# A 1 KB store of expert 0's first values, issued on GpSimd's DMA ring ahead of the full store

## The chip, the cores and the metric

One Trainium2 chip, one of its cores. The metric is the device time of one execution in microseconds (us). The kernel before takes 183.33 us (median of 5 runs, 183.1 to 183.47). A change of the median under about 0.2% (0.37 us) can't be told from no change here.

## What is computed

Eight experts, each a two-layer network with a ReLU between, for 256 rows each:

```python
n_experts, capacity, hidden, expert_hidden = 8, 256, 512, 2048
h = np.matmul(x, w1)      # (8, 256, 512) x (8, 512, 2048)
h = np.maximum(h, 0)
return np.matmul(h, w2)   # (8, 256, 2048) x (8, 2048, 512), float32
```

All inputs and the output are float32 in HBM. w1 and w2 are 4 MB each for every expert, 64 MB in all; the output is 4 MB.

## The kernel before

**Loads.** Each expert's w1 and w2 goes from HBM to SBUF in one DMA (`load_w1`, line 70; `load_w2`, line 76), which turns float32 into bf16 on the way, so 4 MB are read and 2 MB written (2048 KB in the profile). The last two experts' w2 come in pieces: w2(6) in two halves, w2(7) in six pieces of 5, 4, 3, 2, 1 and 1 sixteenths. w1 and w2 have three buffers each, so w1(3) may be loaded only when the first layer of expert 0 has used w1(0), and so on. Nearly all of these, the x of the last four experts and all stores but the last expert's, are issued by GpSimd (POOL in the profile) and share one ring, q0 in the profile. The x of the first four experts goes through SP's queue at the start, and the last expert's result through SP's and ACT's queues at the end (lines 194 and 195).

**Work.** For each expert TensorE transposes x (line 86; the copies of the result are lines 93 and 95), does the first layer (line 105, 64 matmuls, whose results ACT and DVE bring through the ReLU into SBUF in turns, lines 115 and 113), then the second layer (line 125, 32 matmuls into two PSUM tiles). DVE copies the first of the two to the output tile (line 136), ACT the second (line 137). An output tile holds two experts, 1 MB; there are three such buffers. `store` (line 140) writes one from SBUF to HBM.

**Order.** The order on every engine is the order of the calls, written out by hand (lines 143 to 195). GpSimd's instructions run in that order, and a DMA that must wait holds up every one behind it. The scheduler puts in the waits; DMAs from GpSimd take eight completion semaphores in turn, so a DMA also waits until the one eight before it has landed. The calls around the change are these, with their issue in the order of the ring:

```python
    first_layer(0)
    load_w1(3)
    transpose_x(1)
    second_layer(0)
    load_w2(3)        # line 163
    first_layer(1)
    load_w1(4)
    transpose_x(2)
    second_layer(1)
    load_w2(4)
    store(0, 1)       # line 169
    first_layer(2, ...)
    load_w1(5)        # line 171
```

So the ring holds, in order: w1(0), w2(0), w1(1), w2(1), x of experts 4 to 7, w1(2), w2(2), w1(3), w2(3), w1(4), w2(4), store(0, 1), w1(5), w1(6), w1(7), w2(5), store(2, 3), the two halves of w2(6), the six pieces of w2(7), store(4, 5), store(6).

Of the kernel before, what the change touches and what calls it, by code (L numbers as in the profile page):

```python
# [10 lines left out]
def kernel(  # L11
# [7 lines left out]
    nc = tc.nc  # L19
# [20 lines left out]
    out_r = out.rearrange("e (p mt) n -> p e mt n", p=P)  # L40
# [11 lines left out]
    w1_sb, w2_sb, ht, o_sb = {}, {}, {}, {}  # L52
# [19 lines left out]
    def load_w2(e):  # L72
        w2_sb[e] = wpool.tile([P, KT2, H], bf, tag="w2", name="w2_sb")
        cuts = {E - 2: (0, 8, 16), E - 1: (0, 5, 9, 12, 14, 15, 16)}.get(e, (0, KT2))
        for lo, hi in zip(cuts, cuts[1:]):
            nc.gpsimd.dma_start(w2_sb[e][:, lo:hi, :], w2_r[e, :, lo:hi, :])  # L76

    def transpose_x(g, kts=range(KT1)):


        n = GROUPS[g][1]
        J = n * MT
        for kt in kts:
            pt = ps_o.tile([P, J, P], bf, tag="ps_o", name="pt_tr")
            for j in range(J):
                nc.tensor.transpose(pt[:, j, :], x_b[g][:, j, kt::KT1], identity[:])  # L86
            src = pt[:].rearrange("p (j m) (e l) -> p m e l j", m=MT, e=n)
            for mt in range(MT):
                dst = xt[g][:, kt, :, mt * P:(mt + 1) * P].rearrange(
                    "p e (l j) -> p e l j", j=J // MT  # L90
                )
                if mt % 2:
                    nc.scalar.copy(dst, src[:, mt])  # L93
                else:
                    nc.vector.tensor_copy(dst, src[:, mt])  # L95

    def first_layer(e, between=()):
        g = group_of[e]
        xe = xt[g][:, :, e - GROUPS[g][0], :]
        ht[e] = hpool.tile([P, KT2, C], bf, tag="ht", name="ht_sb")  # L100
        for q in range(KT2 // 2):
            ph = ps_h.tile([P, 2, C], f32, tag="ps_h", name="pt_h")
            for i in range(2):
                for kt in range(KT1):
                    nc.tensor.matmul(  # L105
                        ph[:, i, :],
                        w1_sb[e][:, kt, 2 * q + i::KT2],
                        xe[:, kt, :],
                        start=(kt == 0),
                        stop=(kt == KT1 - 1),  # L110
                    )
            if q % 2:
                nc.vector.tensor_relu(ht[e][:, 2 * q:2 * q + 2, :], ph[:])  # L113
            else:
                nc.scalar.activation(ht[e][:, 2 * q:2 * q + 2, :], ph[:], relu)  # L115
            if q % 2 and between:
                between.pop(0)()

    def second_layer(e):
        po = [  # L120
            ps_o.tile([P, H], f32, tag="ps_o", name=f"pt_o{mt}") for mt in range(MT)
        ]
        for kt in range(KT2):
            for mt in range(MT):
                nc.tensor.matmul(  # L125
                    po[mt][:],
                    ht[e][:, kt, mt * P:(mt + 1) * P],
                    w2_sb[e][:, kt, :],
                    start=(kt == 0),
                    stop=(kt == KT2 - 1),  # L130
                )
        es = next(es for es in STORES if e in es)
        if e == es[0]:
            o_sb[es] = opool.tile([P, 2, MT, H], f32, tag="o", name="out_sb")
        o = o_sb[es][:, e - es[0]]
        nc.vector.tensor_copy(o[:, 0, :], po[0][:])  # L136
        nc.scalar.copy(o[:, 1, :], po[1][:])  # L137

    def store(*es):
        nc.gpsimd.dma_start(out_r[:, es[0]:es[-1] + 1], o_sb[es][:, :len(es)])  # L140


    nc.sync.dma_start(x_f[:, :2], x[0:2].rearrange("e (p mt) k -> p e mt k", p=P))
# [16 lines left out]
    load_w1(3)  # L160
    transpose_x(1)
    second_layer(0)
    load_w2(3)
    first_layer(1)
    load_w1(4)
# [3 lines that stand above are left out]
    store(0, 1)  # L169
    first_layer(2, [lambda kt=kt: transpose_x(3, [kt]) for kt in range(KT1)])  # L170
    load_w1(5)
# [5 lines left out]
    load_w1(7)  # L177
    load_w2(5)
    store(2, 3)
    load_w2(6)  # L180
    second_layer(4)
# [5 lines left out]

    second_layer(5)
    store(4, 5)
    second_layer(6)  # L190
    store(6)
# [34 lines left out]
```

## Time and profile before

| | before |
|---|---|
| median of 5 runs | 183.33 us (183.1 to 183.47) |
| the profiled execution: its time | 183.47 us |
| its span, first to last instruction | 181.3 us |
| PE busy | 127.4 us (70%) |
| DVE, ACT, POOL busy | 32.8, 33.9, 15.8 us |
| moved by DMA | 41.01 MB, mean 226 GB/s |
| mean granted TensorE clock | 0.945 |

The profile is of one execution on the chip; times in it count from the start of its span. Busy time of an engine leaves out waits. A DMA has an issue (the instruction on POOL, SP or ACT) and a landing (its completion); "DMA to landing" is the time between the start of the one and the other, so a landing's time is the issue's start plus that. Where DMAs stand in one ring, the distance from one landing to the next is the time that the later one took of the ring. The chain of work that ended last follows what released each step, back from the end.

### The profile page before, as it was taken

Reading aid. Unit: us, or ns where it says so; the run is one execution under the profiler, and the core shown is the slowest. Engines: PE = TensorE matmul, PEld = TensorE weight load, DVE = VectorE, ACT = ScalarE, POOL = GpSimd, SP = SyncE. Lnnn points to the kernel's source line nnn. Section 1 sums busy time; section 2 is a strip of 40 time slices with the busy share of each in tenths; the row PEclk is TensorE's granted clock in tenths of the full one; section 3 lists DMA queues with packets and bytes.
Section 4 is the critical chain, followed back from the end, with each engine's and each line's share of the span. In section 5 each row is a group of like instructions: output and inputs, shape, how many; then the busy total and the mean of one; then the engine's idle time right before and its main releaser. Section 6 shows DMA issues by size and latency. Waiting matters only on the chain.

```text
span 181.3 us, 1891 instructions
## 1 busy us (share of the span) xinstructions
PE 127.4 (70%) x832; PEld 89.8 (50%) x832; DVE 32.8 (18%) x56; ACT 33.9 (19%) x61; POOL 15.8 (9%) x33
## 2 busy tenths in 40 slices
PE   0200898979690299969987692925979498997980
PEld 0100685469340189427933681404969386443430
DVE  0100023033401025211311130010324123010110
ACT  2403323023301025111301130011223022010110
POOL 7200001010102000100010006011010101110100
PEclk9999999999999579996999999996999979999996
DMA  6998998999899989998999899999999999999994
GB/s 187 333 260 202 231 231 174 231 231 231 175 230 231 231 174 231 231 231 174 231 231 228 177 231 296 229 213 228 202 224 213 228 199 310 229 212 213 206 350 176
DMA packets 4984, 41.01 MB, mean 226 GB/s; under 512 B 496, under 2 KB 752, under 8 KB 2672
## 3 DMA queue, kind: packets, MB, share of 16 engines
q0 software_dynamic: 4272, 38.27, 95.6%
q1 hardware_dynamic: 560, 2.36, 3.6%
q10 hardware_dynamic: 144, 0.26, 0.4%
q8 instruction: 6, 0.10, 0.2%
q14 instruction: 2, 0.02, 0.0%
HBM read 71.30 MB, written 4.19 MB: 416 GB/s over the span
## 4 chain that ended last, share of the span: by engine, by line
DMA 44%; PE 42%; another core or an unknown queue 8%; issue 1%; ACT 1%; POOL 1%; DVE 1%; POOLq 0%
DMA w_sb<-in_w_dram 44%; PE pt_o L125 23%; PE pt_h L105 18%; PE pt_tr L86 1%; ACT xt L93 1%; DVE ht_sb L113 0%; ACT out_sb L137 0%; POOL w_sb L76 0%; POOL w_sb L70 0%; DVE xt L95 0%; POOL identity masks.py:199 0%; POOL identity masks.py:197 0%; POOLq L210 0%
## 5 line engine op out<-in xcount | busy, mean ns | idle before, releaser
L105 PE MATMUL pt_h<-xt,w_sb 128*128 128x256 bf16 x512 | 67.2, 299 | 32.9 <-DMA w_sb<-in_w_dram 21.9
L105 PEld LDWEIGHTS <-w_sb 128*128 128x128 bf16 x512 | 60.9, 148 | 39.9 <-DMA w_sb<-in_w_dram 35.1
L125 PE MATMUL pt_o<-w_sb,ht_sb 128*128 128x512 bf16 x256 | 56.6, 379 | 9.1 <-DMA w_sb<-in_w_dram 6.8
L125 PEld LDWEIGHTS <-ht_sb 128*128 128x128 bf16 x256 | 24.9, 98 | 39.1 <-issue 8.9
L113 DVE TENSOR_SCALAR ht_sb<-pt_h 128x512 bf16<-128x512 f32 x32 | 22.1, 692 | 78.6 <-PE pt_h L105 78.6
L115 ACT ACTIVATE ht_sb<-pt_h 128x512 bf16<-128x512 f32 x32 | 19.1, 598 | 60.3 <-PE pt_h L105 60.3
L137 ACT COPY out_sb<-pt_o 128x512 f32<-128x512 f32 x8 | 4.7, 586 | 61.0 <-PE pt_o L125 61.0
L136 DVE COPY out_sb<-pt_o 128x512 f32<-128x512 f32 x8 | 5.5, 692 | 58.1 <-PE pt_o L125 58.1
L76 POOL DMA_DIRECT2D w_sb<-in_w_dram x14 | 7.6, 541 | 58.6 <-DMA w_sb<-in_w_dram 33.2
L70 POOL DMA_DIRECT2D w_sb<-in_w_dram x8 | 4.5, 558 | 82.8 <-PE pt_h L105 51.0
L86 PE MATMUL pt_tr<-identity,x_b 128*128 128x128 bf16 x64 | 5.1, 231 | 6.7 <-ACT x_b L153 6.7
L86 PEld LDWEIGHTS <-x_b 128*128 128x128 bf16 x64 | 4.6, 117 | 6.8 <-ACT x_b L153 6.7
L95 DVE COPY xt<-pt_tr 128x128 bf16<-128x128 bf16 (+2 forms) x16 | 5.6, 382 | 7.1 <-PE pt_tr L86 7.1
L93 ACT COPY xt<-pt_tr 128x128 bf16<-128x128 bf16 (+2 forms) x16 | 5.2, 378 | 8.1 <-DVE xt L95 8.1
L140 POOL DMA_DIRECT2D out_dram<-out_sb x4 | 2.7, 678 | 13.2 <-ACT out_sb L137 12.9
L156 ACT CAST x_b<-x_f 128x1024 bf16<-128x1024 f32 x2 | 2.0, 1042 | 8.9 <-DMA x_f<-in_x_dram 8.9
L153 ACT CAST x_b<-x_f 128x1024 bf16<-128x1024 f32 x1 | 1.0, 1044 | 3.6 <-DMA x_f<-in_x_dram 3.6
L153 ACT ACT_TABLE_LOAD x1 | 1.3, 1283 | 0.7 <-PEq L210 0.7
L154 ACT CAST x_b<-x_f 128x1024 bf16<-128x1024 f32 x1 | 1.0, 1042 | 0.0
L66 POOL DMA_DIRECT2D x_b<-in_x_dram x1 | 0.6, 558 | 0.0
masks.py:199 POOL TENSOR_SCALAR_AFFINE_SELECT identity<-identity 128x128 bf16<-128x128 bf16 x1 | 0.3, 290 | 0.1
masks.py:197 POOL MEMSET identity<- 128x128 bf16 x1 | 0.2, 224 | 0.0
(4 smaller groups left out, 0.4 us busy)
## 6 DMA issues: line engine op xcount, KB each, us to landing
w_sb<-in_w_dram POOLq DMA_DIRECT2D x14, 2048.0 KB, 47.8
out_dram<-out_sb POOLq DMA_DIRECT2D x3, 1024.0 KB, 46.0
x_f<-in_x_dram SPq DMA_DIRECT2D x2, 1024.0 KB, 10.1
w_sb<-in_w_dram POOLq DMA_DIRECT2D x2, 1024.0 KB, 51.6
x_b<-in_x_dram POOLq DMA_DIRECT2D x1, 1024.0 KB, 48.5
w_sb<-in_w_dram POOLq DMA_DIRECT2D x1, 640.0 KB, 49.1
w_sb<-in_w_dram POOLq DMA_DIRECT2D x1, 512.0 KB, 46.5
out_dram<-out_sb POOLq DMA_DIRECT2D x1, 512.0 KB, 9.0
```

Of the source, the lines that this page charges most:

```text
L70: nc.gpsimd.dma_start(w1_sb[e][:], w1_r[e])
L76: nc.gpsimd.dma_start(w2_sb[e][:, lo:hi, :], w2_r[e, :, lo:hi, :])
L86: nc.tensor.transpose(pt[:, j, :], x_b[g][:, j, kt::KT1], identity[:])
L93: nc.scalar.copy(dst, src[:, mt])
L95: nc.vector.tensor_copy(dst, src[:, mt])
L105: nc.tensor.matmul(ph[:, i, :], w1_sb[e][:, kt, 2 * q + i::KT2], xe[:, kt, :], start=(kt == 0), stop=(kt == KT1 - 1),)
L113: nc.vector.tensor_relu(ht[e][:, 2 * q:2 * q + 2, :], ph[:])
L115: nc.scalar.activation(ht[e][:, 2 * q:2 * q + 2, :], ph[:], relu)
L125: nc.tensor.matmul(po[mt][:], ht[e][:, kt, mt * P:(mt + 1) * P], w2_sb[e][:, kt, :], start=(kt == 0), stop=(kt == KT2 - 1),)
L136: nc.vector.tensor_copy(o[:, 0, :], po[0][:])
L137: nc.scalar.copy(o[:, 1, :], po[1][:])
L140: nc.gpsimd.dma_start(out_r[:, es[0]:es[-1] + 1], o_sb[es][:, :len(es)])
```

## The change

One more DMA is issued on GpSimd, between second_layer(0) and load_w2(3): 16 partitions by 16 float32 values (64 bytes of each partition) of expert 0's first output half go from the output tile to the same place in HBM where store(0, 1) writes them again later. So that the two writes can't cross, store(0, 1) is made to wait until the small one has landed.

```diff
     def store(*es):
-        nc.gpsimd.dma_start(out_r[:, es[0]:es[-1] + 1], o_sb[es][:, :len(es)])
+        d = nc.gpsimd.dma_start(out_r[:, es[0]:es[-1] + 1], o_sb[es][:, :len(es)])
+        if 0 in es:
+            tc.add_manual_dep(
+                d.ins,
+                early.ins.name,
+                mybir.DependencyInfo(
+                    mybir.DependencyClass.Sync, mybir.DependencyReason.SCHED_ONLY
+                ),
+                reason="overwrites it",
+            )
...
     second_layer(0)
+    early = nc.gpsimd.dma_start(out_r[0:16, 0, 0, 0:16], o_sb[(0, 1)][0:16, 0, 0, 0:16])
     load_w2(3)
```

In the built program, PE, DVE, ACT and SP have the same instructions in the same order as before. POOL has one more. Its waits are: the small store waits for DVE's copy (line 136 for expert 0); store(0, 1) now also waits for the small store's landing and, because the turn of the semaphores has moved by one, for the landing of x of experts 4 to 7; the second-layer copies of expert 6 on DVE and ACT, which take over store(0, 1)'s buffer, wait for the small store too. The DMAs behind store(0, 1) keep their own waits or move to one that an earlier DMA of the same ring had already met.

## The prediction, made before the changed kernel was run

> **What bounds the kernel.** I read the page's DMA part first: is the ring ever short of work?
>
> ```profile
> DMA  6998998999899989998999899999999999999994
> q0 software_dynamic: 4272, 38.27, 95.6%
> ```
>
> The 16 DMA engines are busy in every slice, and GpSimd's ring (q0) alone fills 95.6% of their span. PE is busy for 70%. So the ring is the limit; what counts for the end is how much time a DMA takes of the ring, not when it was issued, as long as it is issued before the ring comes to it. Next, POOL's part of the timeline gives the issues around the change (columns: start, duration, engine, line, and in brackets the idle time before with its releaser).
>
> ```profile
> 29.06 0.54 POOL L70 DMA_DIRECT2D w_sb<-in_w_dram  x1 [23.38 <-PE pt_tr L86]
> 37.34 0.53 POOL L76 DMA_DIRECT2D w_sb<-in_w_dram  x1 [7.74 <-PE pt_o L125]
> 45.55 0.53 POOL L70 DMA_DIRECT2D w_sb<-in_w_dram  x1 [7.68 <-PE pt_tr L86]
> 55.10 0.53 POOL L76 DMA_DIRECT2D w_sb<-in_w_dram  x1 [9.03 <-PE pt_o L125]
> 55.94 0.71 POOL L140 DMA_DIRECT2D out_dram<-out_sb  x1 [0.30 <-issue]
> 72.79 0.56 POOL L70 DMA_DIRECT2D w_sb<-in_w_dram  x1 [16.14 <-PE pt_h L105]
> 91.01 0.53 POOL L70 DMA_DIRECT2D w_sb<-in_w_dram  x1 [17.66 <-PE pt_h L105]
> ```
>
> In order these are w1(3), w2(3), w1(4), w2(4), store(0, 1), w1(5), w1(6). The view of one line in a window around one issue gives its time to landing; here w1(3) and then store(0, 1):
>
> ```profile
> L70 POOL DMA_DIRECT2D w_sb<-in_w_dram x1: 536/536/536, 29.1 to 29.1; - x1
> DMA to landing us min/median/max: 52.7/52.7/52.7
> ```
>
> ```profile
> L140 POOL DMA_DIRECT2D out_dram<-out_sb x1: 714/714/714, 55.9 to 55.9; - x1
> DMA to landing us min/median/max: 58.6/58.6/58.6
> ```
>
> Every DMA waits some 50 us in the ring behind others. From the same view for each: w2(2) lands at 5.11 + 66.9 = 72.0, w1(3) at 29.06 + 52.7 = 81.8, w2(3) at 37.34 + 54.1 = 91.4, w1(4) at 45.55 + 55.6 = 101.15, w2(4) at 55.10 + 56.9 = 112.0, store(0, 1) at 55.94 + 58.6 = 114.5, w1(5) at 72.79 + 51.4 = 124.2. One 2048 KB load takes 9.7 us of the ring, the store 2.5. Last, the end of the chain that ended last:
>
> ```profile
> 109.24 44.00 DMA w_sb<-in_w_dram
> 153.24 0.04 issue
> 153.28 7.07 PE pt_o L125 x32
> 160.34 0.25 another core or an unknown queue
> 160.60 0.04 issue
> 160.64 3.61 PE pt_o L125 x16
> 164.25 1.20 another core or an unknown queue
> 165.45 0.04 issue
> 165.50 10.58 PE pt_o L125 x48
> 176.08 0.02 issue
> 176.10 0.59 ACT out_sb L137
> ```
>
> The 44 us are w2(5)'s way through the ring. PE then stops for 0.25 and 1.20 us, and starts at once when each half of w2(6) has landed: the second half was issued at 112.30 and took 53.2, so 165.5. After that PE runs 10.58 us without a stop. So **the end is the landing of w2(6)'s second half plus 10.58 us of PE and the last copy and store**. Whatever the ring loses before 165.5 is added to the end one for one; a ring that gained more than 1.20 + 0.25 us would find PE in the way.
>
> **The change, part by part.**
>
> *The small store's issue on POOL.* It waits for DVE's copy of expert 0, which the timeline has at 36.86 for 0.69, so until 37.55; load_w2(3) went at 37.34 before. The other issues take 0.53 to 0.71 us, so w2(3) is issued at about 37.55 + 0.25 of release + 0.6 = 38.4, some 1.1 us later. The ring comes to it when w1(3) is done, at 81.8: 43 us of cover. The next issue, w1(4), waits for PE until 45.55 and isn't touched. Cost 0; without the cover it would be 1.1 us.
>
> *The small store in the ring.* It stands between w1(3) and w2(3) and takes ring time of every DMA engine it uses. No row has a 1 KB DMA. The nearest: the last two 128 KB pieces of w2(7) land at 153.52 + 21.2 = 174.7 and 156.03 + 19.4 = 175.4, the piece before them at 143.83 + 30.2 = 174.0, so each takes 0.70 us; by bytes it should be 9.7 x 128/2048 = 0.61. So 0.1 us goes with being a DMA at all. x of experts 4 to 7 (1024 KB) says the same: it lands 4.9 us after w2(1), and half of 9.7 is 4.85. Bounds: from 0 (what two landings can hide in their rounding) to 0.7, if the smallest DMA seen is a floor. I take **0.1**, since both rows have it, and nothing but the bytes differs.
>
> A rule that speaks against the change stands in the Trainium skill, page "DMA: Bandwidth & Descriptors", section Specifications: pieces under 512 bytes are not moved at line rate but by a read-modify-write. The same page (section "Anatomy of one DMA") puts a fixed 2.0 us on a DMA, most of it the receipt of the write. If that fixed part held the ring, the sum would be +2.0 us; the landings above, 0.1 over the bytes, say that it overlaps with what follows for large pieces, and no row here shows pieces of 64 bytes to HBM.
>
> *The wait of store(0, 1).* It now waits for the small store's landing, just behind w1(3)'s: 81.8 + 0.1 = 81.9 instead of 55.94. Behind it on POOL stands w1(5), then issued at about 82.6 instead of 72.79; w1(6) waits for PE until 91.01 as before. The ring reaches the store at 112.0, when w2(4) is done: 30 us of cover; w1(5) needs the ring at 114.5: 32 us. Cost 0; uncovered, it would be the 26 us of delay. Its other new wait, x of experts 4 to 7, is met at 4.06 + 48.5 = 52.6. The copies of expert 6 on DVE and ACT come after 168 us, when the small store has long landed: 0. All that comes later keeps its waits in substance: 0.
>
> *Sum.* 181.3 + 0.1 = 181.4 of span; with the 183.47 - 181.3 = 2.2 us around it 183.57 for the profiled execution, which lay 0.14 above the median. So the median goes from 183.33 to **183.4**.
>
> **The rivals.**
>
> *The first write to the output costs something, and the small store takes it over more cheaply.* The ring has two odd intervals. w2(4), the load right before the first store, took 112.0 - 101.15 = 10.85 us, 1.15 over the rest; a window set on each shows it:
>
> ```profile
> 91.10:100.80 9.70, 7.07 (x32) 3.03 (x31) 1.03 (x2) 0.59 (x1) 0.44 (x1) 1.00 1.01 216
> 100.80:111.70 10.90, 7.21 (x64) 7.04 (x65) 2.77 (x4) 2.39 (x4) 2.32 (x4) 1.00 1.01 235
> ```
>
> Nothing of the kind stands before store(2, 3): w2(5) landed 9.7 after w1(7). If the surplus belongs to a first write, 1 KB may pay less of it than 1 MB. At most the whole 1.15 is saved: 183.33 + 0.1 - 1.15 = 182.3; half of it: 182.9. Against it: w1(1) lands at 38.0, 10.65 after w2(0) (2.47 + 24.9 = 27.4), with no store in sight, so a surplus of 1 us has other causes too; and POOL issues four DMAs in a row from 108.72 in just that stretch, which the change leaves alone.
>
> *The small store stalls the ring itself (slower).* One mechanism: on each DMA engine a 64-byte write to HBM holds the ring until it is through, between w1(3) and w2(3), at 81.8. Its price from the rows: the 0.7 of the smallest DMA, or the 1.15 of the ring's surplus beside the first store, if that is what a first write costs and it comes twice. 183.33 + 0.7 = 184.0, with both the 0.1 and 1.15, 184.6. It decides from 0.37 us on, as no cover stands between the ring and the end. For it: pieces of 64 bytes are not in the profile at all. Against: store(0, 1) itself has no stall behind it, as w1(5) lands 9.7 after it.
>
> *The wait of store(0, 1) drains the ring (slower).* This needs the small store to land after 112, 30 us later than its place in the ring. Price then: all of what it is late. I see nothing for it.
>
> *Nothing comes of it,* as the small store is too small to see: that is the forecast with 0 for 0.1, and the same case.
>
> **How the numbers follow.** Forecast (0 to 0.3 us more, 183.2 to 183.7 with the spread of medians): 0.42. The first write's cost moved and reduced: 0.25, faster by over 0.2%. The small store's stall: 0.31, and the drained ring 0.02: slower. So faster 0.25, same 0.42, slower 0.33, and 183.4 as the likeliest. Range: to 184.6, the slow rival's upper price; below to 182.5, which takes in three quarters of the saving. What it leaves out is the rest of the saving and of the drained ring, about 0.15. The forecast's own range is 183.2 to 183.7.
>
> **What would show it.** Right: w1(3) lands at 81.8 and w2(3) 9.7 to 9.9 us later; POOL issues store(0, 1) at about 82 and w1(5) right behind; w2(4) keeps its 10.85; w2(6)'s second half lands at 165.5 to 165.7. The faster rival: w2(4)'s interval falls to about 9.7, w2(3)'s grows by less. The slower: w2(3) takes 10.4 us or more and nothing is given back. The forecast is wrong from the start if w2(3)'s or w2(4)'s interval moves by more than 0.4 us.

## The result, and the profile after

The changed kernel takes 182.90 us (median of 32 runs, 182.62 to 183.61), the kernel before 183.33 us (median of 55). The ratio is 0.998, 95% interval [0.9975, 0.9986]: faster by about 0.2% (0.43 us), where 0.1 us more was forecast.

The first surprise is in two numbers. The profiled execution of the changed kernel took 183.20 us, with this first line of its page:

```profile
span 181.4 us, 1893 instructions
```

The span is 0.1 us longer than before (181.3), and so the execution should be 0.1 us slower; yet it is 0.27 faster. 183.20 - 181.41 leaves 1.79 us around the span, where before 183.47 - 181.30 left 2.17. Within the span everything went as forecast. The DMA rows of the page, first:

```profile
DMA  5998998999899989998999898999999999999994
q0 software_dynamic: 4304, 38.28, 95.5%
```

The ring is as full as before; it has 32 packets more (4304 against 4272), one of 64 bytes and one of 4 bytes on each of 16 DMA engines; the trace has such a 4-byte packet on every engine for each of the ring's DMAs (432 for 27 before), and the sixteen of 64 bytes took 24 ns each. POOL's timeline around the change (start, duration, engine, line, idle time before with its releaser):

```profile
27.79 0.54 POOL L70 DMA_DIRECT2D w_sb<-in_w_dram  x1 [22.11 <-PE pt_tr L86]
36.57 0.51 POOL L172 DMA_DIRECT2D out_dram<-out_sb  x1 [8.24 <-DVE out_sb L136]
37.07 0.55 POOL L76 DMA_DIRECT2D w_sb<-in_w_dram  x1
47.33 0.53 POOL L70 DMA_DIRECT2D w_sb<-in_w_dram  x1 [9.71 <-PE pt_tr L86]
56.03 0.53 POOL L76 DMA_DIRECT2D w_sb<-in_w_dram  x1 [8.16 <-PE pt_o L125]
82.70 0.72 POOL L140 DMA_DIRECT2D out_dram<-out_sb  x1 [26.14 <-DMA out_dram<-out_sb]
83.41 0.56 POOL L70 DMA_DIRECT2D w_sb<-in_w_dram  x1
```

The small store is the second row. store(0, 1) now stands idle for 26.14 us, released by the small store's landing, and w1(5) goes right behind it, both some 10 to 27 us later than before. w1(5) lands at 83.41 + 40.9 = 124.31 (before 124.19), so this costs nothing beyond the 0.1 us by which the whole chain lies later. The view of the small store's line in the changed kernel:

```profile
L172 POOL DMA_DIRECT2D out_dram<-out_sb x1: 512/512/512, 36.6 to 36.6; - x1
DMA to landing us min/median/max: 45.4/45.4/45.4
```

It lands at 36.57 + 45.4 = 81.97. By the same view w1(3) lands at 27.79 + 54.0 = 81.79, w2(3) at 37.07 + 54.4 = 91.47, w1(4) at 47.33 + 53.9 = 101.23, w2(4) at 56.03 + 56.1 = 112.13, store(0, 1) at 82.70 + 31.9 = 114.60. The views of w1(3) and of w2(3) in the changed kernel, and of w2(3) before:

```profile
L70 POOL DMA_DIRECT2D w_sb<-in_w_dram x1: 536/536/536, 27.8 to 27.8; - x1
DMA to landing us min/median/max: 54.0/54.0/54.0
```

```profile
L76 POOL DMA_DIRECT2D w_sb<-in_w_dram x1: 554/554/554, 37.1 to 37.1; - x1
DMA to landing us min/median/max: 54.4/54.4/54.4
```

```profile
L76 POOL DMA_DIRECT2D w_sb<-in_w_dram x1: 528/528/528, 37.3 to 37.3; - x1
DMA to landing us min/median/max: 54.1/54.1/54.1
```

w2(3) stands 9.68 us behind w1(3), exactly as before (91.44 - 81.76). Over the profiled executions of all the kernels of this document but the one with many pieces, the distance is 9.67 to 9.78 in the nine without a store there and 9.68 to 9.79 in the four with the 1 KB store. So the small store takes none of the ring's time that landings can show. The long interval of w2(4) is still there as well, 10.90 us; the windows of the changed kernel over w1(4) and w2(4) (columns as before: the stretch, its length, each engine's busy time, clock, DMA share, GB/s):

```profile
91.10:100.80 9.70, 7.07 (x32) 3.03 (x31) 0.69 (x1) 0.59 (x1) 0.00 (x0) 1.00 1.01 216
100.80:111.70 10.90, 7.21 (x64) 7.04 (x65) 2.77 (x4) 2.39 (x4) 2.32 (x4) 0.96 0.99 230
```

And the last rows of the chain that ended last:

```profile
165.56 0.04 issue
165.60 10.56 PE pt_o L125 x48
176.16 0.02 issue
176.18 0.59 ACT out_sb L137
```

From w2(5)'s issue on (109.26, before 109.24) it is row by row the chain of before, up to 0.1 us later. Nothing in it could make the kernel faster. What is left is the time around the span.

### The profile page after: what moved, and what is told of

It reads as the page before. It is cut to its first block, busy times and chain, and to the rows that moved or that the text cites. A ratio compares the mean times of both kernels' runs of the same rounds, so it can differ in the third digit from the quotient of the medians.

```text
span 181.4 us, 1893 instructions
## 1 busy us (share of the span) xinstructions
PE 129.4 (71%) x832; PEld 90.0 (50%) x832; DVE 32.8 (18%) x56; ACT 33.9 (19%) x61; POOL 16.3 (9%) x34
## 3 DMA queue, kind: packets, MB, share of 16 engines
q0 software_dynamic: 4304, 38.28, 95.5%
## 4 chain that ended last, share of the span: by engine, by line
DMA 44%; PE 42%; another core or an unknown queue 8%; issue 1%; POOL 1%; DVE 1%; ACT 1%; POOLq 0%
DMA w_sb<-in_w_dram 44%; PE pt_o L125 23%; PE pt_h L105 18%; PE pt_tr L86 1%; DVE ht_sb L113 0%; ACT out_sb L137 0%; POOL w_sb L76 0%; POOL w_sb L70 0%; ACT xt L93 0%; DVE xt L95 0%; POOL identity masks.py:199 0%; POOL identity masks.py:197 0%; POOLq L220 0%
## 5 line engine op out<-in xcount | busy, mean ns | idle before, releaser
L105 PE MATMUL pt_h<-xt,w_sb 128*128 128x256 bf16 x512 | 66.3, 296 | 30.1 <-DMA w_sb<-in_w_dram 19.1
L105 PEld LDWEIGHTS <-w_sb 128*128 128x128 bf16 x512 | 60.2, 148 | 36.8 <-DMA w_sb<-in_w_dram 32.3
L125 PE MATMUL pt_o<-w_sb,ht_sb 128*128 128x512 bf16 x256 | 59.3, 391 | 9.9 <-DMA w_sb<-in_w_dram 8.6
L125 PEld LDWEIGHTS <-ht_sb 128*128 128x128 bf16 x256 | 25.6, 100 | 42.0 <-issue 15.1
L140 POOL DMA_DIRECT2D out_dram<-out_sb x4 | 2.7, 681 | 39.1 <-DMA out_dram<-out_sb 26.1
L172 POOL DMA_DIRECT2D out_dram<-out_sb x1 | 0.5, 512 | 8.2 <-DVE out_sb L136 8.2
## 6 DMA issues: line engine op xcount, KB each, us to landing
out_dram<-out_sb POOLq DMA_DIRECT2D x3, 1024.0 KB, 31.9
```

The lines of the kernel that those rows point to most:

```text
L105: nc.tensor.matmul(ph[:, i, :], w1_sb[e][:, kt, 2 * q + i::KT2], xe[:, kt, :], start=(kt == 0), stop=(kt == KT1 - 1),)
L125: nc.tensor.matmul(po[mt][:], ht[e][:, kt, mt * P:(mt + 1) * P], w2_sb[e][:, kt, :], start=(kt == 0), stop=(kt == KT2 - 1),)
L140: d = nc.gpsimd.dma_start(out_r[:, es[0]:es[-1] + 1], o_sb[es][:, :len(es)])
```

## The experiments

### Is the gain outside the span, and which part of the change brings it?

**Theory A:** the span is unchanged, and the time around it has fallen. **Theory B:** the one pair of numbers from before is a stray, and the gain lies in the span. Every run has a time and a span, so the two can be told apart by repeating both kernels and by taking the change apart.

The kernel before, unchanged:

> The kernel before, unchanged, to have several of its executions with their spans. Ratio 1.000 to itself within 0.1%. Theory A (the 0.43 us of the changed kernel lie outside the span, since its profiled pair 183.20 / 181.41 leaves 1.79 us around the span where the one pair of before, 183.47 / 181.30, leaves 2.17): the executions here have 2.15 us or so around a span of 181.1 to 181.2. Theory B (the gain lies in the span, and the one pair of before is a stray): 1.8 us around a span of about 181.5.

Measured: 183.41 us, ratio to the other runs of itself 1.0007 [0.9994, 1.0019]; median span 181.2, and in its 12 runs 2.12 to 2.22 us around it, median 2.17. Over the 89 runs of the kernel before that stood beside the experiments: median span 181.1, around it 2.11 to 2.24, median 2.17; the experiments ran on three chips, and on each of them the kernel before has 2.17 or 2.18. Spans are given to 0.1 us, which is most of that width.

The changed kernel, unchanged:

> The changed kernel, unchanged, on the same chip as the two that take it apart. Both theories: 0.998 (0.997 to 0.999), span about 181.1, 1.8 us around it.

Measured: 182.87 us, ratio 0.9984 [0.997, 0.9998]; median span 181.1, around it 1.74 to 1.83, median 1.78. In the 33 runs of the changed kernel's own result it is 1.74 to 1.84, median 1.79, with the same span of 181.1. **Theory A holds**: the spans agree, and the 0.38 us between 2.17 and 1.79 accounts for the gain, which is 0.35 to 0.43 us by the medians of the times. The two ranges don't touch.

The small store without the wait of store(0, 1):

```diff
     second_layer(0)
+    early = nc.gpsimd.dma_start(out_r[0:16, 7, 0, 0:16], o_sb[(0, 1)][0:16, 0, 0, 0:16])
     load_w2(3)
...
-    nc.sync.dma_start(out_r[:, 7, 0, :], o[:, 0, 0, :])
+    d = nc.sync.dma_start(out_r[:, 7, 0, :], o[:, 0, 0, :])
+    tc.add_manual_dep(d.ins, early.ins.name, ..., reason="waits for it")
```

> The small store alone: the same 16 by 64 bytes at the same place in the ring, but to expert 7's rows in HBM, which the last store on SP overwrites some 90 us later (that one waits for it, at no cost). store(0, 1) and w1(5) are issued early again. If the store itself or its place in the ring brings the gain: 0.998. If the later issue of store(0, 1) and w1(5) brings it: 1.000 or 1.001 (the ring's 0.1 us).

Measured: 183.21 us, ratio 1.0002 [0.999, 1.0013]; span 181.2, around it 2.01 to 2.07, median 2.04.

The wait without the small store:

```diff
-    load_w1(3)
+    early = load_w1(3)       # load_w1 returns its DMA
...
     def store(*es):
+        if 0 in es: add_manual_dep(d.ins, early.ins.name, ..., reason="waits for it")
```

> The wait alone: no small store; store(0, 1) waits until w1(3) has landed (81.8), so that it and w1(5) are issued at about 82 and 83 as in the changed kernel. If the later issue brings the gain: 0.997 to 0.998, since the ring's 0.1 us is not paid either. If the small store brings it: 1.000.

Measured: 183.20 us, ratio 0.9997 [0.9986, 1.0008]; span 181.2, around it 1.99 to 2.10, median 2.02.

Neither part gives the gain: each run came out as if the other part brought it, so both accounts missed. But both moved the time around the span, to values of their own, 2.04 and 2.02. So in these kernels it is a property of the program, steady from run to run, and it moves while the spans agree. What these programs differ in, apart from the ring, is the number of instructions, waits counted, in POOL's stream. The page's instruction counts and the trace's records of each engine show it: 1891 before, 60 of them on POOL; 1893 in the changed kernel, 62 on POOL (the store and one more wait, where the part on the change counts the store alone); 1893 with the store alone (61 on POOL, and one more wait on SP); 1890 with the wait alone (59 on POOL, one wait fewer).

### Is it the length of POOL's stream?

**Theory L:** the time around the span goes with the length of POOL's stream, whatever the instructions are. **Theory S:** it goes with the small store, its DMA, its turn of semaphores or its wait. The test adds memsets, instructions that fill a tile with a value; here the tile is one value that nothing reads, so they do nothing for the result and touch no DMA:

```diff
     identity = const.tile([P, P], bf, name="identity")
+    spare = [const.tile([1, 1], f32, name=f"spare{i}") for i in range(2)]
...
     make_identity(nc, identity)
+    for t in spare:
+        nc.gpsimd.memset(t[:], 0.0)
```

> The kernel before with two memsets of one value each on POOL, beside the identity at the start: no DMA, no wait, no store; POOL's stream is as long as in the changed kernel, two instructions more than before. Theory L (what changed is the time outside the span, and it goes with the length of POOL's stream of instructions): time 182.9, 1.8 us around a span of 181.1. Theory S (it goes with the small store, its DMA or its wait): 183.2 to 183.4, 2.17 us around.

Measured: 183.01 us, ratio 0.9987 [0.9975, 0.9999]; median span 181.2, around it 1.76 to 1.84, median 1.80. **Two empty memsets bring what the small store brought.** The first line of its page has the same count as the changed kernel, with no small store in it; the profiled execution was one with a long span, 0.8 us over the median of before:

```profile
span 181.9 us, 1893 instructions
```

Its time was 183.66, so again 1.78 around: what happens in the span comes and goes by some tenths from run to run, and the time around it doesn't follow.

One memset, `range(1)`:

> The same with one memset: POOL's stream has one instruction more than before, as in the kernel with the small store but without store(0, 1)'s wait. Theory L: 2.04 us around the span, as there, or some other value than 2.17; span 181.1. Theory S: 2.17.

Measured: 183.23 us, ratio 0.9998 [0.9987, 1.001]; around the span 2.00 to 2.12, median 2.08, beside 2.04 of the small store alone, which also has one more on POOL.

Four memsets, `range(4)`:

> The same with four memsets: four instructions more than before. Theory L: the time around the span moves again, to a value not yet seen between 1.7 and 2.3, with a span of 181.1. Theory S: 2.17.

Measured: 183.23 us, ratio 0.9998 [0.9989, 1.0008]; around the span 1.93 in the median, 1.90 to 2.12. It is a new value, as theory L said, but any value from 1.7 to 2.3 would have done.

The changed kernel with the two memsets added:

> The changed kernel, small store and wait kept, with the same two memsets: POOL's stream is four instructions longer than before. Theory L: the time around the span is that of the kernel before with four memsets, whatever that is, and no longer 1.8 if that differs. Theory S: 1.8 us around, time 182.9.

Measured: 183.10 us, ratio 0.9996 [0.9986, 1.0006]; around the span 1.96 in the median, 1.72 to 2.17, a wider scatter than the others have. The small store and its wait are all there, yet the time can't be told from that of the kernel before, and 0.17 of the 0.38 us around the span is gone: the kernel has 1.96 as the one with four memsets has 1.93. Theory S falls on both sides, the gain without the store, and the store and its wait without the whole gain. With four more on POOL the runs of one kernel scatter, so here the medians agree and not the single runs.

Eight memsets, `range(8)`:

> The kernel before with eight memsets of one value on POOL at the start. Theory L, as the runs so far leave it: the time around the span goes with the length of POOL's stream, without a steady direction (2.17, 2.05, 1.80 and 1.95 for 0, 1, 2 and 4 instructions more), so some value from 1.7 to 2.3, span 181.1 to 181.3. Theory M (each instruction moves it one way): under 1.8.

Measured: 183.48 us, ratio 1.0004 [0.9994, 1.0014]; around the span 2.24 to 2.34, median 2.29, span 181.2. So the length can cost as well; it is no steady slope, and theory M falls.

Two memsets on DVE instead, `nc.vector.memset`:

> The same as the kernel with two memsets on POOL, but on DVE, so that POOL's stream is as before. If the length of POOL's stream alone counts: 2.17 us around a span of 181.1, time 183.3. If any engine's stream counts: another value than 2.17.

Measured: 183.18 us, ratio 0.9993 [0.9981, 1.0004]; around the span 2.11 to 2.24, median 2.19, as in the kernel before. DVE's stream doesn't count, POOL's does. The small store alone has one more on SP too, and agrees with the one memset, which has not; PE's and ACT's streams were not tried.

All of them by what POOL's stream has more than before:

| more on POOL | kernel | instructions in all | median time | median span | around the span |
|---|---|---|---|---|---|
| -1 | the wait alone | 1890 | 183.20 | 181.2 | 2.02 |
| 0 | before | 1891 | 183.27 (89 runs) | 181.1 | 2.17 |
| 0 | two memsets on DVE | 1893 | 183.18 | 181.0 | 2.19 |
| 1 | the small store alone | 1893 | 183.21 | 181.2 | 2.04 |
| 1 | one memset | 1892 | 183.23 | 181.2 | 2.08 |
| 2 | the change | 1893 | 182.90 | 181.1 | 1.79 |
| 2 | two memsets | 1893 | 183.01 | 181.2 | 1.80 |
| 4 | four memsets | 1895 | 183.23 | 181.3 | 1.93 |
| 4 | the change and two memsets | 1895 | 183.10 | 181.1 | 1.96 |
| 8 | eight memsets | 1899 | 183.48 | 181.2 | 2.29 |

Medians of kernels with the same length agree within 0.04 us, whatever their instructions are; the lengths differ by up to 0.5. The number of instructions in all doesn't order them: the four kernels with 1893 have 1.79, 1.80, 2.04 and 2.19. What is read off the last column is not read off the time alone: a median of ten runs moves by 0.1 to 0.2 with the span.

### Do 64-byte pieces stall the ring?

The slower rival priced a stall of a write of 64 bytes. The small store made large, in pieces of the same size, to expert 7's rows (the last store on SP waits for it, store(0, 1) does not):

```diff
+    def pieces(t):
+        return t.rearrange("p (a b) -> p a b", b=32)[:, :, 0:16]
+    early = nc.gpsimd.dma_start(pieces(out_r[:, 7, 0, :]), pieces(o_sb[(0, 1)][:, 0, 0, :]))
     load_w2(3)
...
```

> The small store made 128 times as large in pieces: 2048 pieces of 64 bytes (128 on each DMA engine in place of 1), to expert 7's rows, with no wait of store(0, 1). If a 64-byte piece passes like other small packets, w2(3) lands some 3 us later against w1(3) (128 times the 20 to 30 ns that a piece would take) and the span grows by the same 3 us. [...] If only the first one stalls, it is the 3 us, since the small store alone gave nothing to see.

Measured: 184.24 us, ratio 1.0049 [1.0034, 1.0064]; median span 182.15, 1.05 over before, and 2.08 around it, which fits its one more on POOL. The view of the new DMA's line in this kernel:

```profile
L165 POOL DMA_DIRECT2D out_dram<-out_sb x1: 1179/1179/1179, 38.4 to 38.4; - x1
DMA to landing us min/median/max: 44.7/44.7/44.7
```

It lands at 38.41 + 44.7 = 83.11. w1(3) landed at 29.63 + 52.3 = 81.93 and w2(3) at 39.58 + 53.0 = 92.58, so 10.65 us apart in place of 9.68: 0.97 us for 128 pieces on each DMA engine, 8 ns a piece. That is a third of the 3 us expected, which took each piece at the duration of a whole small packet. A stall of the slower rival's lower price, 0.7 us, for each piece would be some 90 times as much. The end of the chain in this kernel shows where it goes:

```profile
166.21 10.54 PE pt_o L125 x48
```

PE starts the last stretch at 166.21 instead of 165.50: time lost by the ring does reach the end, as the prediction had it. That is 0.71 later in this execution and not 0.97: w2(4), the load ahead of store(0, 1), took 112.67 - 102.31 = 10.36 here and not 10.85. Whether the pieces did that is not shown, since the wait alone, without any pieces, has 10.36 too.

### Whose is the long interval of w2(4)?

The faster rival rested on it. store(0, 1) put behind w1(5):

```diff
-    store(0, 1)
     first_layer(2, ...)
     load_w1(5)
+    store(0, 1)
```

> store(0, 1) is issued after w1(5) in place of before it, so the first write of the output stands behind w1(5) in the ring, some 10 us later. If the 1.15 us that w2(4) takes more belong to the first large store, w2(4) lands 9.7 us after w1(4) and w1(5) takes 10.8. If they belong to that time (to POOL's four DMAs in a row at 108.7), w2(4) keeps 10.85 and w1(5) 9.7. Span 181.1 either way.

Measured (one run, 183.41 us): w2(4) lands at 55.27 + 55.6 = 110.87, 9.76 after w1(4) (45.71 + 55.4 = 101.11); w1(5) lands at 72.88 + 48.8 = 121.68, 10.81 after w2(4). The views of w2(4) and w1(5) in this kernel:

```profile
L76 POOL DMA_DIRECT2D w_sb<-in_w_dram x1: 528/528/528, 55.3 to 55.3; - x1
DMA to landing us min/median/max: 55.6/55.6/55.6
```

```profile
L70 POOL DMA_DIRECT2D w_sb<-in_w_dram x1: 531/531/531, 72.9 to 72.9; - x1
DMA to landing us min/median/max: 48.8/48.8/48.8
```

In this execution the surplus has moved with the store, to the load ahead of it, and away from POOL's four DMAs in a row, which still start at 108.72 in this kernel. In the thirteen executions with the store in its old place w1(5) took 9.58 to 9.73. So the rival had the place right for this store. But the surplus is no fixed price of a first store. w2(4) took 10.36 to 10.90 in twelve of the thirteen, and 9.94 in the change with two memsets. w2(5), the load ahead of store(2, 3), took 9.62 to 9.72 in twelve of all fourteen, but 10.72 with two memsets (109.14 + 44.9 = 154.04 after 108.62 + 34.7 = 143.32) and 10.32 in the change with two memsets; w1(7) before it took 9.3 in both. And w1(1), with no store in sight, took 10.45 to 10.75 in every one. In the two profiled executions of the changed kernel the small store did not take the surplus over (10.90 and 10.79), nor did it alone (10.75); the 9.94 stands in a kernel that has it too. What the ring waits for in these places is open.

## Why the prediction was wrong

**The step that failed** is the last of the sum: "with the 183.47 - 181.3 = 2.2 us around it". It carried the time around the span over unchanged, and gave it neither bounds nor a rival. It was 1.79 in the changed kernel against 2.17 before. That is 0.38 of the 0.50 us between the forecast 183.4 and the measured 182.90; the 0.1 forecast for the small store in the ring, which the landings don't show, is nearly all the rest. Every term before it held within its bounds:

- *The issue on POOL:* w2(3) was forecast some 1.1 us later and without a cost. It went at 37.07, no later at all in that execution (the small store was issued at 36.57; in the change with two memsets w2(3) went at 38.25, near the forecast's 38.4), and landed when it had landed before.
- *The small store in the ring:* 0.1 us taken, within 0 to 0.7. Measured from w1(3) to w2(3): 9.68 before and after, so the lower end, 0. The pieces of w2(7) that gave 0.1 misled a little.
- *The wait of store(0, 1):* forecast at 82 and w1(5) right behind, cost 0. They went at 82.70 and 83.41, and with the wait alone the median span was 181.2.
- *The span:* 181.4 forecast, 181.4 in the profile, 181.1 in the median, where before has 181.1 too.

*The rivals.* No stall of the small store was seen: it moved no landing, and many such pieces took 8 ns each. The drained ring didn't come. The faster rival's half price, 182.9, is the measured time to the digit, and **its mechanism is not the one that acted**: w2(4)'s interval, which it said would fall to 9.7, is 10.90. That the number fits is luck; without the landing times beside it, it would have been taken for a proof.

Could the view have shown it? No view of the trace of before reaches outside the span, and the one pair (183.47, 181.30) says nothing on what the 2.17 depends on. But a forecast of 0.1 us on a kernel with 2.17 us that no view explains should have kept that term open, by a tenth or two at least.

What stays open is why the length of POOL's stream acts so, in no steady direction, and on which side of the span. The Trainium skill, page "Runtime: NRT & Kernel Launch", section "The launch sequence", says that barriers and semaphore resets by the runtime stand ahead of the kernel and behind it. A program might meet such work in a better or worse position; that is a guess. The same page, section "Instruction fetch mechanics", says that a taken branch to a target outside the two blocks at hand waits for a fetch. If there is such a branch around the span, a place in the instruction stream could cost time; that is a guess as well. No run here shows either.

## What to carry to other kernels

When a change is worth a few tenths of a microsecond, compare spans as well as times: a difference that the spans don't show is not the work's, and any other edit that lengthens the same engine's stream by as much may bring it or take it away, as two memsets on GpSimd did here and two on DVE did not. To test that, add as many instructions that do nothing on the engine that got the new ones. And in a ring with tens of microseconds of work ahead, an issue that came 10 or 27 us later cost nothing here, as it still came some 30 us before the ring reached it; only the ring's own time counted.

## What the runs showed of the hardware that was not expected

- The time around the span went with the number of POOL's instructions: 2.02, 2.17, 2.04 to 2.08, 1.79, 1.93 to 1.96 and 2.29 us for -1, 0, 1, 2, 4 and 8 more; two more on DVE left it at 2.19.
- The load ahead of the first 1 MB store mostly took 0.7 to 1.2 us more of the ring than the others (10.36 to 10.90 against 9.7 in twelve of thirteen executions, 9.94 in one), and in the one execution with the store a load later the surplus stood there. Loads elsewhere show it too: w1(1) always (10.45 to 10.75), w2(5) in two of fourteen (10.72, 10.32).
- A store of 1 KB on a busy ring took no time that its neighbours' landings show, and 2048 pieces of 64 bytes took 0.97 us; the ring of that kernel has 4320 packets against 4272, so the trace counts far fewer packets than pieces.
